# Repacing the load, norm and transposes of x, and moving small copies from VectorE to ScalarE, in a streaming-encoder layer

## The chip, the cores and the metric

The kernel runs on one core of one Trainium2 chip. The metric is the device time of one execution in microseconds. Before the change three runs gave 3767.56, 3769.85 and 3772.0 us, so the median is 3769.85 us.

## The reference, cut to what matters

One layer over 4096 tokens of width 1024, in float32. The input is normalised and projected once; half of the projected columns feed a differential softmax attention (group A), the other half an RWKV-7 recurrence (group B); both are gated, joined, projected and added to the input.

```python
xn = rms_norm(h, norm_g[l]); proj = xn @ w_in[l]
# group A: four heads, block-causal
p = softmax(q1 k1) - lam * softmax(q2 k2);  o_a = p @ v
# group B: eight heads; token shift of r, k, v, decay and a inputs
rwkv_in = z + (prev(z) - z) * shift_mu
# state S (64 x 64 per head), token by token
S_t = S_{t-1} diag(w_t) + (S_{t-1} (-kk_t)) (kk_t * a_t)^T + v_t k_t^T;  y_t = S_t r_t
h = h + concat([o_a, o_b]) @ w_out[l]
```

## The kernel before, in words

There are three phases. Phase 1 projects x and runs the recurrence, phase 2 is the attention, phase 3 the output projection. The change touches phase 1 alone.

Phase 1 walks over eight blocks of 512 tokens, in the order r0 a0 r1 a1 r2 a2 r3 r4 r5 r6 r7 a7 a6 a5 a4 a3, where r is the recurrence's share of the columns and a the attention's. A block's normalised, transposed input is held as a high part xh and a low part xl, so each product is three matmuls (mm3). Each letter is a row of jobs. A token-major job (VB and GB of r, V and GA of a) runs tm_part twice (L264), 16 steps each, a step being the three matmuls of one of eight weight tiles; its first part makes output rows of tokens 0 to 255 of the block, its second part those of 256 to 511. In each part two outputs s0 and s0+1 are interleaved, the second lagging by two steps. A feature-major job (fm_groups) takes 8 or 16 steps. Weight tiles come from a ring of eight; a tile's release, in part two of a token-major job, issues the load of the tile eight further on. After the first pass the weights come from a kept copy in DRAM (L233).

x for the next block is brought in beside the jobs: x_load (L148) loads two tiles into a ring of two buffers, x_norm (L157) squares them on ScalarE, takes the rsqrt on GpSimd and scales them on ScalarE, x_trans (L168) transposes them in four groups on TensorE (L176), and each group is evicted by ScalarE to xh (L179) and by VectorE to xl (L180). The first half of a block is normed and transposed in the last job before the block (x_norm0, x_half0), the second half in the block's first job (x_half1); `paced` (L317) runs each piece after given steps of the job.

Beside the projections run four streams, written as generators: p1_stream prepares units of 256 tokens (decay, keys, bonus; GpSimd makes rk at L506, TensorE the bonus sum from it at L524), p2_stream builds the chunk matrices and inverts them (the elimination on VectorE at L578 and L579, then the matmuls pz L594 and ptt L613 with copies Zs and TT), c_stream carries the state over chunks of 64 tokens (px L687, copy xs L690, pu L695, pst L716, state L725 and L728), o_stream finishes the output. The token shift of r, k and the LoRA columns is made in ev_shift (L285): ScalarE scales, VectorE adds the shifted rest, the first column from the carry and saves the last column as the new carry.

TensorE's instructions stand in the order in which the code issues them. After every step of the projections `tick` (L924) gives each stream a turn; a yield of n waits n beats, a negative yield also waits for a beat divisible by four (G). The other engines and SP's DMA queue are ordered by the framework's scheduler.

Of the kernel before, what the change touches and what calls it, by code (L numbers as in the profile page):

```python
# [12 lines left out]
AF = mybir.ActivationFunctionType  # L13
ALU = mybir.AluOpType
# [11 lines left out]
W = dict(  # L26
    G=4,    xn=2, xl=1024, sw=1024, np=2, le=3, l0=8, gb=5, pj=3, sb=4, wb=8, tb1=7, wm=0,
    xw=2048, cw=512, pl=1, pelat=330, tb=3, pb=3, lag2=2.0, ms=40, a0=2, a1=2, a2=2, a3=2,
    a4=2, a5=2, a6=2, a7=2, a8=2, a9=2, b0=2, b1=2, b2=2, b3=2, b4=2, b5=2,
    b6=2, b7=2, b8=1, b9=1, c0=10, c1=8, c2=2, c3=2, c4=1, c5=1, c6=2, c7=3,  # L30
    c8=2, o0=2, o1=4, o2=2, o3=4, o4=2, o5=2, o6=1, held=5, el=1, pz=18, ld=14,
    ba=2,  df=[2, 2, 2, 2],
# [76 lines left out]
def _phase1(ctx, tc, nc, e):  # L109
    x, w_in, norm_g, shift_mu = e["x"], e["w_in"], e["norm_g"], e["shift_mu"]  # L110
    S, D, KD, NB, NU = e["S"], e["D"], e["KD"], e["NB"], e["NU"]
# [34 lines left out]
    xraw = {}  # L146

    def x_load(b, t):  # L148
        xs = []
        for s in range(2):  # L150
            r0 = b * BT + t * 256 + s * 128
            xv = xp.tile([128, D], F32, tag="xv", name="xv", bufs=2)
            nc.sync.dma_start(xv, x[r0:r0 + 128, :])
            xs.append(xv)
        xraw[b, t] = xs
# [28 lines left out]
    jobs, tiles, first_tile = [], [], []  # L184
# [56 lines left out]
    def release(n):  # L241
        assert n == nuse[0], (n, nuse[0])
        nuse[0] += 1
        wt.pop(n)
        prep()

    def mm3(po, ah, al, bh, bl, k):
        nc.tensor.matmul(po, ah, bh, start=(k == 0), stop=False)  # L248
        nc.tensor.matmul(po, ah, bl, start=False, stop=False)  # L249
        nc.tensor.matmul(po, al, bh, start=False, stop=(k == KD - 1))  # L250
# [10 lines left out]
                yield  # L261
            evacs[p](po)

    def tm_part(n0, s0, evac, last, side_x):  # L264
        po = {}
        order = []
        for n in range(KD + 2):
            if n < KD:
                order.append((s0, n))
            if n >= 2:  # L270
                order.append((s0 + 1, n - 2))
        for s, k in order:
            if k == 0:
                po[s] = ps_j.tile([128, BT], F32, tag="pj", name="pjt")
            w = wt[n0 + k]
            sl = slice(128 * s, 128 * s + 128)
            mm3(po[s], xh[:, k, sl], xl[:, k, sl], w[:, 0].rearrange("p a c -> p (a c)"), w[:, 1].rearrange("p a c -> p (a c)"), k)
            if k == KD - 1:
                evac(s)(po[s])
            if last and s == s0 + 1:  # L280
                release(n0 + k)
            next(side_x, None)
            yield

    def ev_shift(gi, dst, t0):  # L285
        def f(po):
            o = stg.tile([128, 512], F32, tag="st", name="st")
            nc.scalar.activation(o, po, AF.Copy, scale=om_f[:, gi:gi + 1])
            mu = mu_f[:, gi:gi + 1]
            nc.vector.scalar_tensor_tensor(o[:, 1:512], in0=po[:, 0:511], scalar=mu, in1=o[:, 1:512], op0=ALU.mult, op1=ALU.add)  # L290
            nc.vector.scalar_tensor_tensor(o[:, 0:1], in0=carry[:, gi:gi + 1], scalar=mu, in1=o[:, 0:1], op0=ALU.mult, op1=ALU.add)
            nc.vector.tensor_copy(carry[:, gi:gi + 1], po[:, 511:512])
            nc.sync.dma_start(dst[:, t0:t0 + 512], o)
        return f

# [21 lines left out]
    def paced(g, steps):  # L317
        for n in range(64):
            if n in steps:
                next(g, None)  # L320
            yield

    def x_half1(b):
        x_norm(b, 1)
        yield
        yield from x_trans(b, 1)
        if b == 0:
            xfree[0] = True
            raw_next()

    def x_half0(b):
        yield from x_trans(b, 0)
        x_load(b, 1)
        yield

    def x_norm0(b):
        x_norm(b, 0)
        yield

    def tile_job(i, kind, parts, evs, nxt):  # L340
        n0 = first_tile[i]
        if kind == "f":
            assert not bg
            yield from fm_groups(n0, parts, [ev(0) for ev in evs])
            return
        half1 = bg.pop(1, None)
        assert half1 is None or nxt is None
        if nxt is not None:
            x_load(nxt, 0)
        if half1 is not None:  # L350
            side = paced(x_half1(half1), (4, 6, 8, 10, 12, 13))
        else:
            side = paced(x_norm0(nxt) if nxt is not None else iter(()), (10,))
        yield from tm_part(n0, 0, evs[0], False, side)
        for _ in side:
            pass
        side = paced(x_half0(nxt) if nxt is not None else iter(()), (1, 4, 7, 10, 11))
        yield from tm_part(n0, 2, evs[0], True, side)
        for _ in side:
            pass  # L360
        if nxt is not None:
            bg[1] = nxt
# [29 lines left out]
    order = []  # L392
# [4 lines left out]
    def main():  # L397
        x_norm(0, 0)
        yield from x_trans(0, 0)
        x_load(0, 1)  # L400
        bg[1] = 0
        for _ in range(RING):
            prep()
        for i, (k, parts, evs, nxt, rdone) in enumerate(jobs):
            yield from tile_job(i, k, parts, evs, nxt)
            if rdone:
                done_r[0] += 1
# [127 lines left out]
    def p2_unit(u):  # L535
# [39 lines left out]
        for j in range(31):  # L575
            n, w = 31 - j, j // 2 + 1
# [11 lines left out]
        TT = TTs[u % 2]  # L588
        pz = ps_g.tile([128, 16, 32], F32, tag="pg", name="pz")
        Drf = Dr.rearrange("p c r s -> p s c r")  # L590
        for pc in range(16):
            for h in range(2):
                b0 = 64 * h
# [3 lines left out]
            yield  # L597
        Zs = rq.tile([128, 16, 32], F32, tag="e2", name="Zs", bufs=3)
        nc.scalar.copy(Zs[32:64], pz[32:64])
        nc.vector.tensor_copy(Zs[96:128], pz[96:128])  # L600
        for q in range(4):
            sl = slice(32 * q, 32 * q + 32)
            nc.scalar.copy(TT[sl, :, 32 * (q % 2):32 * (q % 2) + 32], DT[sl])
# [5 lines left out]
        pt = ps_g.tile([128, 16, 32], F32, tag="pg", name="ptt")  # L609
        for pc in range(16):  # L610
            for h in range(2):
                b0 = 64 * h
                nc.tensor.matmul(pt[b0:b0 + 32, pc], Zs[b0 + 32:b0 + 64, pc], DT[b0 + 32:b0 + 64, pc], start=True, stop=True)  # L613
        yield W["b8"]
        nc.scalar.copy(TT[0:32, :, 32:64], pt[0:32])
        nc.vector.tensor_copy(TT[64:96, :, 32:64], pt[64:96])
        yield W["b9"]
        UN[u] = (ARF, WC, BON, RN, GS, bkt, TT)

# [30 lines left out]
    def c_stream():  # L650
# [5 lines left out]
        for ch in range(4 * NU):  # L656
# [3 lines left out]
            ARF, WC, BON, RN, GS, bkt, TT = UN[u]  # L660
# [22 lines left out]
            px, pu, pst = pc[:, 0], pc[:, 1], pc[:, 0]  # L683
# [3 lines left out]
                    nc.tensor.matmul(px[64 * h:64 * h + 64, j], GS[c][:, j, h, 0:64], svu[:, h, j], start=True, stop=True)  # L687
            yield W["c3"]
            xs = rp.tile([128, 4, 64], F32, tag="xs", name="xs", bufs=1)
            nc.vector.tensor_copy(xs, px)  # L690
            yield -W["c4"]
            for j in range(4):
                for h in range(2):
# [90 lines left out]
    def p1_stream():  # L784
        for u in range(NU):
            while done_r[0] * BT < 256 * (u + 1):
                yield 1
            p_load(u)
            yield W["ld"]
            yield from p1_unit(u)  # L790

    def p2_stream():
        for u in range(NU):
            yield from p2_unit(u)

    for n, (kind, b) in enumerate(order):
        ts = tiles_r(b) if kind == "r" else tiles_a(b)
        nb = order[n + 1][1] if n + 1 < len(order) else b
        for m, (cols, w, k, parts, evs) in enumerate(ts):
# [7 lines left out]
            nxt = nb if (m == len(ts) - 1 and nb != b) else None  # L807
# [18 lines left out]
    carry = c1.tile([128, 9], F32, name="carry")  # L826
# [88 lines left out]
    with tc.manual_schedule(engines={mybir.EngineType.PE}):  # L915
        side = [p1_stream(), p2_stream(), c_stream(), o_stream()]
# [535 lines left out]
```

## Time and profile before

| what | us |
|---|---|
| runs, median (of 3) | 3769.85 |
| profiled execution | 3761.58 |
| its span | 3759.9 |
| PE busy | 3609.4 (96%) |
| VectorE (DVE) busy | 2632.4 (70%) |
| ScalarE (ACT) busy | 1922.4 (51%) |
| GpSimd (POOL) busy | 761.2 (20%) |

PE is TensorE's matmuls, PEld its weight loads. An idle time is put down to what ended it: "PE pt L176 <- ACT xv L166" is time in which the transposes into pt waited for ScalarE's scaling of x. The granted clock is given as a share: 1.00 is 2.4 GHz, 0.50 is 1.2 GHz, and a mean in between says that a part of the stretch ran at 1.2 GHz. Phase 1 ends at about 2140 us, phase 2 at about 3600 us.

### The profile page before, as it was taken

What the parts mean: (1) busy time and instruction counts of PE and PEld (TensorE: products, weight loads), DVE (VectorE), ACT (ScalarE), POOL (GpSimd) and SP (SyncE); (2) the same over time, 40 slices, a digit from 0 to 9 for tenths busy, and PEclk for the clock granted to TensorE, in tenths of its full rate; (3) what the DMA queues carried; (4) which work ended last, traced back from release to release, by engine and by line L of the source; (5) the groups of instructions that cost most, each with busy time, mean ns of one, the idle gap of its engine ahead of it and who ended that gap; (6) DMA issues with size and microseconds to landing.
All of it is one profiled execution on the core that took longest, in us unless ns stands there. A gap on an engine that the chain in (4) does not pass through costs nothing.

```text
span 3759.9 us, 69957 instructions
## 1 busy us (share of the span) xinstructions
PE 3609.4 (96%) x26370; PEld 3050.9 (81%) x26370; DVE 2632.4 (70%) x5882; ACT 1922.4 (51%) x4042; POOL 761.2 (20%) x1156
## 2 busy tenths in 40 slices
PE   7999999999999999998999999999999999989999
PEld 5777777777777778777777789999999999978887
DVE  3566666667767787757777588898898898863333
ACT  4452352444445443444444377787787787761111
POOL 0112211211212222212221032222222222211000
PEclk9999999999999999999999999999999999999999
DMA  7976665666555565665675651141141131033332
GB/s 231 354 267 204 209 212 198 222 204 225 192 192 190 191 226 174 215 209 196 221 239 200 204 122 48 41 113 37 49 104 49 38 82 40 21 134 121 134 134 74
DMA packets 346092, 593.60 MB, mean 158 GB/s; under 512 B 55193, under 2 KB 210329, under 8 KB 345754
## 3 DMA queue, kind: packets, MB, share of 16 engines
q1 hardware_dynamic: 344602, 587.62, 48.4%
q8 instruction: 208, 3.41, 0.4%
q10 hardware_dynamic: 1152, 1.51, 0.1%
q14 instruction: 130, 1.06, 0.1%
HBM read 434.85 MB, written 154.14 MB: 157 GB/s over the span
## 4 chain that ended last, share of the span: by engine, by line
PE 75%; DVE 13%; DMA 4%; ACT 3%; issue 2%; SPq 2%; POOL 1%; DVEq 0%; POOLq 0%; ACTq 0%
PE po L1222 12%; PE ps L1127 6%; PE ps L1126 6%; PE tp L1197 6%; PE pjf L248 5%; PE pjf L250 4%; PE pjf L249 4%; PE pjt L248 4%; PE pjt L250 4%; PE pjt L249 4%; PE po L1372 3%; PE po L1371 3%; PE po L1370 3%; DVE DG L578 2%; DVE TL L579 2%
## 5 line engine op out<-in xcount | busy, mean ns | idle before, releaser
L1159 ACT ACTIVATE ring<-ring,nm 128x2048 f32<-128x2048 f32 (+14 forms) x472 | 589.0, 1253 | 31.3 <-DVE nm L1151 30.2
L1141 DVE CUSTOM_DVE_ANT_0 ring<-ps,zcol 128x1024 f32<-128x1024 f32 (+6 forms) x464 | 485.2, 1058 | 109.2 <-PE ps L1127 103.1
L1222 PE MATMUL po<-v,pt 128*128 128x128 f32 x4224 | 539.5, 276 | 10.0 <-ACT pt L1210 5.4
L1222 PEld LDWEIGHTS po<-v,pt 128*128 128x128 f32 x4224 | 517.9, 192 | 28.5 <-ACT pt L1210 7.3
L1126 PE MATMUL ps<-k,ta 128*128 128x512 f32 (+3 forms) x1152 | 483.1, 420 | 7.3 <-DMA ta<-q_d 4.9
L248 PE MATMUL pjt<-w,xh 128*128 128x512 f32 x1024 | 436.2, 426 | 29.1 <-DMA w<-ws_d 13.4
L248 PE MATMUL pjf<-xh,w 128*128 128x512 f32 x1088 | 451.1, 415 | 6.0 <-ACT w L236 4.5
L1127 PE MATMUL ps<-k,tb 128*128 128x512 f32 (+3 forms) x1152 | 432.0, 379 | 0.0
L250 PE MATMUL pjf<-xh,w 128*128 128x512 f32 x1088 | 431.0, 396 | 0.5 <-DVE w L237 0.5
L249 PE MATMUL pjf<-xl,w 128*128 128x512 f32 x1088 | 429.9, 395 | 0.0
L249 PE MATMUL pjt<-w,xh 128*128 128x512 f32 x1024 | 410.5, 401 | 0.9 <-DVE w L237 0.9
L250 PE MATMUL pjt<-w,xl 128*128 128x512 f32 x1024 | 410.0, 401 | 0.1
L1182 DVE SCALAR_TENSOR_TENSOR ring<-ring,rho 128x512 f32<-128x512 f32 (+3 forms) x600 | 407.1, 702 | 1.6
L1210 ACT COPY pt<-tp 128x512 f32<-128x512 f32 (+3 forms) x576 | 303.1, 550 | 194.0 <-PE tp L1197 188.7
L1197 PE MATMUL tp<-ident,ring 128*128 128x128 f32 x2112 | 313.6, 274 | 3.7 <-DVE ring L1182 3.7
L1197 PEld LDWEIGHTS tp<-ident,ring 128*128 128x128 f32 x2112 | 254.6, 142 | 40.6 <-issue 3.7
L248 PEld LDWEIGHTS pjt<-w,xh 128*128 128x128 f32 x1024 | 199.0, 194 | 80.9 <-DMA w<-ws_d 20.3
L248 PEld LDWEIGHTS pjf<-xh,w 128*128 128x128 f32 x1088 | 207.3, 191 | 57.4 <-ACT w L236 6.5
L250 PEld LDWEIGHTS pjf<-xh,w 128*128 128x128 f32 x1088 | 207.0, 190 | 49.2 <-DVE w L237 2.7
L1126 PEld LDWEIGHTS ps<-k,ta 128*128 128x128 f32 x1152 | 219.2, 190 | 32.8 <-issue 5.0
L1127 PEld LDWEIGHTS ps<-k,tb 128*128 128x128 f32 x1152 | 220.1, 191 | 23.4
L249 PEld LDWEIGHTS pjf<-xl,w 128*128 128x128 f32 x1088 | 208.0, 191 | 38.1
(205 smaller groups left out, 6421.4 us busy)
## 6 DMA issues: line engine op xcount, KB each, us to landing
w<-ws_d SPq DMA_DIRECT2D x448, 512.0 KB, 5.3
ws_d<-w SPq DMA_DIRECT2D x64, 512.0 KB, 5.3
xv<-in_x_dram SPq DMA_DIRECT2D x48, 512.0 KB, 5.4
ta<-q_d SPq DMA_DIRECT2D x128, 128.0 KB, 2.9
tb<-q_d SPq DMA_DIRECT2D x128, 128.0 KB, 3.0
k<-k_d SPq DMA_DIRECT2D x32, 512.0 KB, 7.1
mi<-mix_d SPq DMA_DIRECT2D x32, 512.0 KB, 3.3
xi<-in_x_dram SPq DMA_DIRECT2D x32, 512.0 KB, 4.2
```

Of the source, the lines that this page charges most:

```text
L248: nc.tensor.matmul(po, ah, bh, start=(k == 0), stop=False)
L249: nc.tensor.matmul(po, ah, bl, start=False, stop=False)
L250: nc.tensor.matmul(po, al, bh, start=False, stop=(k == KD - 1))
L1126: nc.tensor.matmul(ps[:, c:c + w], rr(ta[:, m, qs]), rr(k[:, m, c:c + w]), start=True, stop=False)
L1127: nc.tensor.matmul(ps[:, c:c + w], rr(tb[:, m, qs]), rr(k[:, m, c:c + w]), start=False, stop=True)
L1141: nc.vector.tensor_tensor_reduce(rg(m, ro, x), st["ps", b, m][:, c - 1024 * b:c - 1024 * b + x], msk, 0.125, -3.0e38, ALU.add, ALU.max, ac ...
L1159: nc.scalar.activation(rg(m, ro, x), rg(m, ro, x), AF.Exp, bias=st["nm"][:, m:m + 1], accum_out=st["lp"][:, m, j:j + 1])
L1182: nc.vector.scalar_tensor_tensor(rg(0, ro, x), in0=rg(1, ro, x), scalar=st["rho"], in1=rg(0, ro, x), op0=ALU.mult, op1=ALU.add)
L1197: nc.tensor.transpose(tp[:, j], rg(0, c, 128), ident)
L1210: nc.scalar.copy(pt[:, :n], st.pop(("tp", g))[:, :n])
L1222: nc.tensor.matmul(st["po"], pt[:, j], vt[h, kb // 8][:, kb % 8], start=(kb == 0), stop=(kb == i))
L1370: nc.tensor.matmul(po, mh[:, k], wh[k][:, fs], start=(k == 0), stop=False)
```

## The change

- The load of the next block's first half is issued one job earlier where the weights of that job come from the kept copy, and its norm then runs after step 3 of the job instead of step 10. Its transposes run after steps 0, 3, 5 and 8 of part two instead of 1, 4, 7 and 10, and the second half's load after 9 instead of 11.
- The second half's norm runs after step 5 instead of 4 and its transposes after steps 12, 14, 17 and 20 of the job instead of 6, 8, 10 and 12 (for the first block as before).
- Part two of a token-major job lags its second output by four steps instead of two.
- The yield before the bonus matmul (a8) is 5 instead of 2.
- Four kinds of small operations go from VectorE to ScalarE: the copy xs, the first column and the carry in ev_shift, and the second halves of the copies Zs and TT.

```diff
-    a4=2, a5=2, a6=2, a7=2, a8=2, a9=2, b0=2, b1=2, b2=2, b3=2, b4=2, b5=2,
+    a4=2, a5=2, a6=2, a7=2, a8=5, a9=2, b0=2, b1=2, b2=2, b3=2, b4=2, b5=2,
...
-    def tm_part(n0, s0, evac, last, side_x):
+    def tm_part(n0, s0, evac, last, side_x, lag):
...
-        for n in range(KD + 2):
+        for n in range(KD + lag):
             if n < KD:
                 order.append((s0, n))
-            if n >= 2:
-                order.append((s0 + 1, n - 2))
+            if n >= lag:
+                order.append((s0 + 1, n - lag))
...
-            nc.vector.scalar_tensor_tensor(o[:, 0:1], in0=carry[:, gi:gi + 1], scalar=mu, in1=o[:, 0:1], op0=ALU.mult, op1=ALU.add)
-            nc.vector.tensor_copy(carry[:, gi:gi + 1], po[:, 511:512])
+            nc.scalar.activation(o[:, 0:1], carry[:, gi:gi + 1], AF.Identity, scale=mu, bias=o[:, 0:1])
+            nc.scalar.copy(carry[:, gi:gi + 1], po[:, 511:512])
...
+        if half1 is not None:
+            side = paced(x_half1(half1), (5, 12, 14, 17, 20, 21) if half1 else (4, 6, 8, 10, 12, 13))
+        elif nxt is not None:
+            if (nxt, 0) not in xraw:
+                x_load(nxt, 0)
+                side = paced(x_norm0(nxt), (10,))
+            else:
+                side = paced(x_norm0(nxt), (3,))
+        else:
+            side = iter(())
+        yield from tm_part(n0, 0, evs[0], False, side, 2)
         if nxt is not None:
-            x_load(nxt, 0)
-        if half1 is not None:
-            side = paced(x_half1(half1), (4, 6, 8, 10, 12, 13))
-        else:
-            side = paced(x_norm0(nxt) if nxt is not None else iter(()), (10,))
-        yield from tm_part(n0, 0, evs[0], False, side)
-        for _ in side:
-            pass
-        side = paced(x_half0(nxt) if nxt is not None else iter(()), (1, 4, 7, 10, 11))
-        yield from tm_part(n0, 2, evs[0], True, side)
+            for _ in side:
+                pass
+            side = paced(x_half0(nxt), (0, 3, 5, 8, 9))
+        yield from tm_part(n0, 2, evs[0], True, side, 4)
...
         for i, (k, parts, evs, nxt, rdone) in enumerate(jobs):
+            if i + 1 < len(jobs) and jobs[i + 1][3] is not None and not tiles[min(first_tile[i + 1], len(tiles) - 1)][3]:
+                x_load(jobs[i + 1][3], 0)
...
-        nc.vector.tensor_copy(Zs[96:128], pz[96:128])
+        nc.scalar.copy(Zs[96:128], pz[96:128])
...
-        nc.vector.tensor_copy(TT[64:96, :, 32:64], pt[64:96])
+        nc.scalar.copy(TT[64:96, :, 32:64], pt[64:96])
...
-            nc.vector.tensor_copy(xs, px)
+            nc.scalar.copy(xs, px)
```

## Rows read from the trace of the kernel before

**Rows 1.** Table by windows, phase 1: stretch, length, busy us of each engine, clock, DMA.
```profile
220.00:2140.00 1920.00, 1827.27 (x15083) 1476.65 (x15081) 1322.98 (x2967) 802.83 (x1806) 412.56 (x410) 0.98 0.63 207
```

**Rows 2.** PE's waits, 220 to 2140: who waited for whom, us, times, longest.
```profile
PE pt L176 <- ACT xv L166: 19.8, 15, 4.1
PE pjt L248 <- DMA w<-ws_d: 13.4, 12, 2.9
PE pbn L524 <- POOL rr L506: 13.3, 3, 5.2
PE pt L176 <- DVE xl L180: 11.9, 5, 4.5
PE pjt L248 <- DVE st L311: 11.7, 7, 4.0
```

**Rows 3.** Table by windows, slices of 20 us around waits for x and rk.
```profile
500.00:520.00 20.00, 17.32 (x87) 14.41 (x85) 18.47 (x50) 14.60 (x34) 3.14 (x6) 0.89 0.75 278
...
1400.00:1420.00 20.00, 16.15 (x185) 13.13 (x186) 10.03 (x19) 10.10 (x25) 4.13 (x4) 0.83 0.37 122
1620.00:1640.00 20.00, 19.70 (x142) 16.16 (x143) 8.87 (x15) 11.24 (x29) 1.41 (x3) 0.87 0.52 152
1960.00:1980.00 20.00, 16.64 (x126) 13.54 (x125) 17.97 (x41) 7.56 (x18) 3.30 (x2) 0.91 0.70 239
```

**Rows 4.** Timeline, PE and ACT, 502 to 517: start, us, engine, line, operation.
```profile
502.88 0.60 PE L176 MATMUL pt<-ident,xv 128*128 128x128 f32 x4
...
514.00 0.33 PE L176 MATMUL pt<-ident,xv 128*128 128x128 f32 x1 [0.37 <-ACT xv L166]
515.41 1.17 ACT L166 ACTIVATE xv<-xv,rs 128x1024 f32<-128x1024 f32 x1
516.63 0.90 PE L176 MATMUL pt<-ident,xv 128*128 128x128 f32 x3 [2.30 <-ACT xv L166]
```

**Rows 5.** Groups by line and shape, DVE and ACT, 0 to 2140: busy, mean ns, idle before.
```profile
L690 DVE COPY xs<-pc 128x256 f32<-128x256 f32 x64 | 26.8, 418 | 31.3 <-PE pc L687 31.0
L291 DVE SCALAR_TENSOR_TENSOR st<-carry,mu_f,st 128x1 f32<-128x1 f32 x72 | 18.1, 252 | 0.0
L600 DVE COPY Zs<-pz 32x512 f32<-32x512 f32 x16 | 11.2, 697 | 84.9 <-ACT Zs L599 84.7
L179 ACT ACTIVATE xh<-pt,g_t 128x256 fp32r<-128x256 f32 x192 | 87.9, 472 | 91.6 <-DVE xl L180 50.6 <-PE pt L176 39.7
L489 ACT ACTIVATE f<-tha,kac,kah 128x256 f32<-128x256 f32 x64 | 35.5, 604 | 0.2
```

**Rows 6.** Timeline, PE, bonus matmuls and pz, 1284 to 1404.
```profile
1284.58 1.87 PE L524 MATMUL pbn<-rks,rr 128*128 128x2 f32 x8 [4.75 <-POOL rr L506]
1291.65 1.98 PE L594 MATMUL pz<-Dr,GS 32*32 32x32 f32 x64 [0.40 <-DVE Dr L586]
1403.85 1.87 PE L524 MATMUL pbn<-rks,rr 128*128 128x2 f32 x8 [5.19 <-POOL rr L506]
```

**Rows 7.** Timeline, ACT and DVE, the two half copies of pz, 542 to 544.
```profile
542.63 0.58 ACT L599 COPY Zs<-pz 32x512 f32<-32x512 f32 x1
543.24 0.70 DVE L600 COPY Zs<-pz 32x512 f32<-32x512 f32 x1 [11.45 <-ACT Zs L599]
```

**Rows 8.** Timeline, ACT and DVE, one eviction of the token shift, 1269 to 1279.
```profile
1269.31 0.67 ACT L288 ACTIVATE st<-pjf,om_f 128x512 f32<-128x512 f32 x1
1278.55 0.75 DVE L290 SCALAR_TENSOR_TENSOR st<-pjf,mu_f,st 128x511 f32<-128x511 f32 x1
```

**Rows 9.** The last chunk, timeline of PE and DVE; then SP's waits: us, times, longest.
```profile
2123.59 0.69 PE L687 MATMUL pc<-svu,GS 128*64 128x64 f32 x16
2132.66 0.87 DVE L728 TENSOR_TENSOR svu<-svu,WC 64x256 f32<-64x256 f32 x2
SPq L1025 <- DVE svu L728: 11.8, 1, 11.8
```

## The prediction

> **What bounds the kernel now.** I read the page's slices first, then the table by windows, then PE's waits, then short timelines around the longest of them. The change touches phase 1 alone (0 to about 2140 us); the stretch after it is written by its own planner and stays as it is. From 220 to 2140 us PE is busy 1827 of 1920 us, with DVE at 1323 and ACT at 803 [rows 1]: PE is the bound, and what can be won is its 93 us of idle time and what it loses at the lower clock. So the question is which waits end last on PE. They are few and named [rows 2]: the transposes of x wait for the normalised x (19.8 us, 15 times) and for a buffer that VectorE's xl frees (11.9), the projections wait for weights (13.4) and for a PSUM buffer that the gate's eviction frees (11.7), and the bonus matmul waits for GpSimd's rk (13.3, three times). A long wait costs twice: in 500 to 520 us the granted clock has a mean of 0.89, and so on in six such 20 us slices around waits for x, of which [rows 3] has the first and the last; 20 us x (1 - clock) over the six (0.89, 0.85, 0.88, 0.95, 0.91, 0.87) is 13.0 us of PE's work lost at 1.2 GHz.
>
> **The order of the work.** PE runs in written order, in beats of three matmuls: a 32-step job of the token-major kind is 32 beats. From the last transposes of one half of x to the first of the next half are 12 beats, and they took 514.00 - 502.88 = 11.1 us [rows 4], so a beat with its share of the side streams is 0.93 us. I use that price for a beat throughout.
>
> **The change, part by part.**
>
> *x repaced.* The second half of x is loaded when the first half's last transposes free its buffers. From those transposes (502.88) to the second scaled tile (515.41 + 1.17 = 516.58) are 13.7 us [rows 4]; the order gives 12 beats = 11.1 us, so PE waits 2.3 us more and loses its clock. Now the first half's last transposes stand at step 8 of part two instead of 10, and the second half's first at step 12 of the next job instead of 6: 20 beats = 18.6 us against 13.7. The wait is covered with 4.9 us to spare, in all ten transitions with this distance. It removes 19.8 + 13.0 = 32.8 us. What is late next: the second half is used from step 16 on, so its transposes at 12, 14, 17, 20 have only 3 to 4 beats (2.8 to 3.7 us) to be evicted, where before they had 10 or more. An eviction is ScalarE 0.472 us [rows 5] and then VectorE, two of each in turn, so about 2 us when nothing stands before them. With VectorE behind, the matmuls wait instead. From below this costs nothing, from above all of the 32.8 comes back; nearest is the case where queues are short, with some 0.8 us lost in each of ten transitions: 8. Net **25**. The earlier load of the first half and its earlier norm I cost at nothing: its transposes are not the ones that wait in [rows 4], and the early DMA stands on SP ahead of stores that it doesn't hold up, since its buffers are free by then. If it did hold SP, later weights would be late (below). The first half's own transposes come in 0, 3, 5, 8, a little denser than before; where they wait for VectorE (11.9 us in [rows 2]) nothing is relieved, **-1**, with -5 and +3 as ends.
>
> *Lag 4 in part two.* The first output of part two ends at step 11 instead of 13 and the second starts two steps later, so an eviction has two beats (1.9 us) more before its buffer is wanted. Of the seven waits for the gate's eviction (11.7 us, the longest 4.0) this can take at most 1.9 each; the longest stand where VectorE is behind and come back at the next wait. Take **+5** of 0 to 11.7. Against it: the weights of the job are released later, the first after step 6 instead of 4, the next job of the same kind uses them from 16 on, so the load has 8 beats (7.4 us) at the tightest place instead of 10. Fifteen such boundaries x 1.9 = 28 us is the upper end, 0 the lower; most of the twelve waits for weights come from SP standing behind stores, not from a late release: **-4**.
>
> *The bonus matmul four beats later (a8).* Slots come at every fourth beat, so the distance from rk to the matmul grows from 6 beats to 10, and for the second pair of heads all stands 8 beats (7.4 us) later. The three waits are 4.75, 5.19 and 3.36 us, so all end. But at 1284.58 the next matmul that needs VectorE's inverse waited 0.40 us right after [rows 6]: there VectorE is the bound, and the 4.75 would be waited out at 1291.65. The other two count: 5.19 + 3.36 = 8.6, and the clock around them (0.83 and 0.91 [rows 3]: 3.4 + 1.8 = 5.2) makes 13.8; **+12** of 0 to 18. The price: all of the inverse and the recurrence moves 8 beats later against the projections. At the end of phase 1 this isn't hidden. Now the last chunk's first matmul is at 2123.59 and its state is done at 2132.66 + 0.87, 1.5 us before the projections end at about 2135 [rows 9]. Shifted by 8 beats, the last two steps of the chain have no projections beside them, and SP's first loads of phase 2 wait for that state (11.8 us at one load, [rows 9]). Ends 0 and 7.4; the chain without its filler matmuls is shorter by some 2, so **-5**. Elsewhere the shift makes new meetings of busy VectorE with x, with either sign; take **-5** of -20 to +10.
>
> *Copies to ScalarE.* VectorE loses 64 copies of xs (26.8 us), 72 first columns (18.1), 16 halves of Zs (11.2), and the like halves of TT and the carries: the three rows alone are 56 us of 1323 [rows 5]. ScalarE gains 64 x 0.472, 32 x 0.58, and 72 x two tiny ones. For the first column with two pointer operands no row exists; it lies between 0 and the 0.604 us of a 256-column activation with two such operands [rows 5], I take 0.4, by that row and its smaller size. All in all under 126 us on an engine that is 42% busy: no bound there. What VectorE wins off PE's path is worth little: **+2**, ends 0 and 8. The half copies stood one after the other already: VectorE's half began at 543.24, when ScalarE's 0.58 us from 542.63 were over [rows 7]. So nothing parallel is given up, and ScalarE's second half is 0.1 us shorter.
>
> The Trainium skill, "PSUM — Partial Sum Buffer", in "PSUM bank collisions raise a hardware error", lets two engines read one bank at once if they are in different quadrants of partitions; by that the halves could have run side by side and the move would cost 16 x 2 x about 0.5 us of the chain. The trace doesn't agree: the halves are strictly one behind the other.
>
> *The wait that is added.* The carry's copy reads the same PSUM tile as VectorE's shift. If ScalarE has to wait for that, its queue stands still, and behind it stand xs, the tanh and exp of the next unit, and the copies for the inverse. One shift began at 1278.55 for a ScalarE eviction that ended at 1269.98: 9.3 us to its end [rows 8]. That is the worst; after most evictions ScalarE is idle for some us anyway. Take **-4**; the ends are 0 and the rival below.
>
> The same section of the Trainium skill keeps any two engines apart on one bank and quadrant, reads against reads too. By that rule this wait exists; [rows 5] has ScalarE's xh waiting 50.6 us for VectorE's xl of the same tile, which agrees.
>
> **Sum.** 25 - 1 + 5 - 4 + 12 - 5 - 5 + 2 - 4 = 25 us. The profiled execution took 3761.58 (span 3759.9), so 3736.6 by it; it lay 8.3 under the median of the runs shown (3769.85), and against that median the forecast is **3745**.
>
> **The rivals.**
>
> *Forecast, 0.55*: 3745, own range 3730 to 3757.
>
> *The wait moves from x to its eviction, 0.18.* The transposes are in time, but the projections wait for xl with the same clock loss. For it: 3 to 4 beats, and VectorE at 18.47 of 20 us in the slice of [rows 3]. Against it: shorter waits. The 25 shrink to 5: 3765.
>
> *ScalarE's queue, slower, 0.13.* The carry's copy holds ScalarE until VectorE's shift, p1's tanh and exp start late, rk is late again and PE waits at the bonus matmul as now at 1403.85. Each such wait costs 5.2 and 3.4 of clock = 8.6 us. Units 7 to 9 have their elimination beside r jobs, six halves: 6 x 8.6 = 52, so 3745 + 52 = 3797. It decides from the third half on (3 x 8.6 = 26 eats the gain). Against it: the matmul stands 4 to 8 beats later. The rule of the Trainium skill above is what makes this rival, and its chance is the 0.13.
>
> *Weights, 0.04.* Lag 4 makes most of the fifteen boundaries wait: 20 of the 28 us are paid, 3761 to 3765.
>
> *All of it comes, 0.10.* No eviction is late and the counter-costs stay near 0: 50 us, 3720.
>
> **How the numbers follow.** A measurement tells 0.2%, 7.5 us, from no change. Faster (under 3762): nearly all of the forecast (0.53), all of the last rival, 0.07 of the second: 0.70. Same: 0.02 of the forecast, 0.09 of the second, the weights, a little of ScalarE's queue: 0.16. Slower: 0.14, from ScalarE's queue and the worst of the second. The range goes from the good case to just beyond no change: 3718 to 3777.
>
> **What would show it.** Right: the waits of PE for the scaled x fall to under 3 us after 220, those for rk to under 3, the mean clock of 220 to 2140 rises, PE's new waits for xl at the projections stay under 10 us in total, and phase 2's first scores start some 5 us later after the projections' end than now. Wrong: waits for xl at the projections of 15 us or more, PE waiting for ScalarE's xs or Zs, ScalarE idle before the carry's copy for long and rk late again, or weights late at the boundaries of token-major jobs.

## The result, and the profile after

The change made the kernel slower: 3789.5 us median (3788.6 to 3790.3) against 3768.7 for the kernel before, ratio 1.0054 [1.0036, 1.0071]. The forecast was 3745 with a range to 3777, so both the sign and the range were missed. The profiled execution has a span of 3786.8 us. Kernels are compared by their ratios below: executions of one kernel lie up to 22 us apart, and the profiled one of before (3761.58) was 8 us under the median of its own, so two traces alone would say +27.

Lines beyond 410 are 7 further down than before (pz is L601, px L694, xs L697); kernels with x's old places keep the old numbers. The table by windows, phase 1 (columns as in [rows 1]):

```profile
220.00:2160.00 1940.00, 1829.55 (x15090) 1473.46 (x15086) 1259.39 (x2739) 869.58 (x2027) 411.76 (x408) 0.97 0.61 204
```

PE does the same work in 20 us more. VectorE lost 64 us of busy time and ScalarE gained 67, as the copies should make it; the mean clock did not rise but fell a little. PE's idle time is 1940 - 1829.6 = 110 us, where [rows 1] has 93. The waits of PE in that stretch tell where it sits (waited for: us, times, longest us):

```profile
PE pjt L248 <- DMA w<-ws_d: 29.5, 26, 3.8
PE pjt L248 <- DVE st L311: 12.5, 5, 4.1
PE pa L465 <- DVE xl L180: 8.4, 4, 2.7
PE pjt L250 <- DVE xl L180: 8.3, 8, 2.0
PE ptt L620 <- ACT Zs L606: 7.4, 3, 4.6
...
PE pt L176 <- DVE xl L180: 5.7, 3, 2.6
PE pjt L248 <- DVE sl L301: 5.2, 1, 5.2
...
PE pjt L248 <- ACT carry L292: 3.7, 1, 3.7
PE pc L702 <- ACT xs L697: 2.8, 1, 2.8
PE pjt L248 <- ACT xh L179: 2.5, 2, 1.6
PE pt L176 <- ACT xv L166: 2.5, 1, 2.5
```

Against [rows 2]: what the change aimed at is gone (x's norm 19.8 to 2.5, rk 13.3 to nothing). In its place stand weights (13.4 to 29.5), x's evictions at the projections and at pa, which is the next unit's inner products (16.7 together, neither of them among the long waits before), the inverse's copies on ScalarE (7.4), and two evictions of projections (sl and carry, 8.9). With the transposes' waits for xl (11.9 to 5.7) these three are 37 us that went. Over all of PE's waits in the two windows 46 us went and 67 came.

The end of phase 1, timeline of PE and DVE (start us, us, engine, line, operation, idle before):

```profile
2154.66 0.39 PE L250 MATMUL pjt<-w,xl 128*128 128x512 f32 x1
...
2157.31 0.69 PE L723 MATMUL pc<-svu,bkt 128*64 128x64 f32 x16 [1.35 <-DVE svu L719]
...
2158.95 0.87 DVE L735 TENSOR_TENSOR svu<-svu,WC 64x256 f32<-64x256 f32 x2
...
2166.34 0.76 PE L1133 MATMUL ps<-k,ta 128*128 128x512 f32 x1 [6.58 <-DMA ta<-q_d]
```

The projections end at 2155.1, 20.0 us later than before (2135.1). The last chunk's state is done at 2158.95 + 0.87 = 2159.8, now behind them, and the first full score matmul of phase 2 starts 11.2 us after the projections' end where it was 5.3. These 6 us are the price that the forecast had put at 5. So the handover came as predicted, and in these two executions the projections were 20 us late instead of early. By the ratio, which has 20 us in all, it is some 14.

The moved copies, groups by line and shape (busy, mean ns, idle before):

```profile
L291 ACT ACTIVATE st<-carry,st,mu_f 128x1 f32<-128x1 f32 x72 | 27.9, 388 | 1.4
...
L697 ACT COPY xs<-pc 128x256 f32<-128x256 f32 x64 | 23.7, 371 | 10.3 <-PE pc L694 9.3
...
L292 ACT COPY carry<-pjf 128x1 f32<-128x1 f32 x72 | 11.3, 157 | 62.5 <-DVE st L290 60.8 <-DVE DG L585 0.3
...
L607 ACT COPY Zs<-pz 32x512 f32<-32x512 f32 x16 | 9.2, 578 | 0.4
```

Beside [rows 5]: xs costs 371 ns for 418, the half of Zs 578 for 697, the first column 388 for 252 (the forecast took 400). The wait that was added is there: ScalarE stood 60.8 us before the carry's copy for VectorE's shift. The Trainium skill, "PSUM — Partial Sum Buffer", in "PSUM bank collisions raise a hardware error", keeps two engines from reading one bank and quadrant together; the trace agrees that the copy waits, and the next section shows that this wait is not what made the kernel slower.

### The profile page after: what moved, and what is told of

The parts are those of the page before. It is cut to its first block, busy times and chain, and to the rows that moved or that the text cites. A ratio compares the mean times of both kernels' runs of the same rounds, so it can differ in the third digit from the quotient of the medians.

```text
span 3786.8 us, 70039 instructions
## 1 busy us (share of the span) xinstructions
PE 3613.9 (95%) x26370; PEld 3048.8 (81%) x26370; DVE 2566.6 (68%) x5642; ACT 1993.0 (53%) x4282; POOL 763.4 (20%) x1156
## 4 chain that ended last, share of the span: by engine, by line
PE 69%; DVE 13%; DMA 5%; ACT 3%; issue 2%; POOL 1%; SPq 0%; DVEq 0%; POOLq 0%; ACTq 0%
PE po L1229 12%; PE ps L1134 6%; PE ps L1133 6%; PE tp L1204 6%; PE pjt L248 4%; PE pjf L248 4%; PE pjt L250 3%; PE pjt L249 3%; PE pjf L250 3%; PE pjf L249 3%; PE po L1379 3%; PE po L1378 3%; PE po L1377 3%; DVE TL L586 2%; DVE DG L585 2%
## 5 line engine op out<-in xcount | busy, mean ns | idle before, releaser
L248 PE MATMUL pjt<-w,xh 128*128 128x512 f32 x1024 | 439.5, 430 | 60.6 <-DMA w<-ws_d 29.5
L250 PEld LDWEIGHTS pjt<-w,xl 128*128 128x128 f32 x1024 | 199.3, 195 | 60.9 <-DVE xl L180 16.4
```

## The experiments

The change has four parts: the copies, x's places, lag 4 and the shift (a8=5, by which the bonus matmul stands 4 beats later and the inverse and the recurrence 8). Eighteen kernels were run. The table gives each one's parts, its ratio to the kernel before, the end of the last projection, and the time from there to the first full score matmul, both in its profiled execution. That one lies up to 7 us from its kernel's median, and 8 under it for the kernel before, so a few us in the column of the last projection tell nothing.

| kernel | copies | x | lag 4 | shift | ratio [95%] | last projection us | to phase 2 us |
|---|---|---|---|---|---|---|---|
| before | | | | | 1 | 2135.1 | 5.3 |
| p_act | yes | | | | 0.9973 [0.9962, 0.9983] | 2131.8 | 5.1 |
| f_x | yes | yes | | | 0.9962 [0.9949, 0.9976] | 2132.5 | 5.2 |
| f_lag | yes | | yes | | 0.9978 [0.9966, 0.9990] | 2131.0 | 4.9 |
| f_a8 | yes | | | yes | 0.9990 [0.9981, 0.9999] | 2133.7 | 12.0 |
| m_a8 | yes | yes | yes | | 0.9968 [0.9957, 0.9979] | 2130.6 | 4.3 |
| m_x | yes | | yes | yes | 0.9979 [0.9970, 0.9988] | 2129.6 | 11.1 |
| m_lag | yes | yes | | yes | 1.0018 [1.0009, 1.0027] | 2148.8 | 11.5 |
| after | yes | yes | yes | yes | 1.0054 [1.0036, 1.0071] | 2155.1 | 11.2 |
| m_act | | yes | yes | yes | 1.0074 [1.0061, 1.0087] | 2164.0 | 11.7 |
| p_x | | yes | | | 1.0007 [0.9995, 1.0020] | 2142.3 | 5.0 |
| p_lag | | | yes | | 1.0004 [0.9992, 1.0016] | 2138.3 | 4.5 |
| p_a8 | | | | yes | 1.0024 [1.0013, 1.0034] | 2145.8 | 11.4 |

**Each part taken out of the full change.** The theory on record was that one part carries the loss. The edits on the changed kernel:

```diff
 m_lag: -    yield from tm_part(n0, 2, evs[0], True, side, 4)
        +    yield from tm_part(n0, 2, evs[0], True, side, 2)
 m_a8:  -a8=5,
        +a8=2,
 m_x:   -(5, 12, 14, 17, 20, 21) if half1 else (4, 6, 8, 10, 12, 13)
        +(4, 6, 8, 10, 12, 13)
        -side = paced(x_half0(nxt), (0, 3, 5, 8, 9))
        +side = paced(x_half0(nxt), (1, 4, 7, 10, 11))
        -                x_load(jobs[i + 1][3], 0)      # the early load
 m_act: -nc.scalar.copy(xs, px)
        +nc.vector.tensor_copy(xs, px)                  # and the other copies likewise
```

> The changed kernel (3789.5 us) with part two's lag at two steps again, all else as changed. Theory W (late weights): lag 4 releases the weights later, and PE's waits for weights grew by 16 us with their clock; then this run is 12 to 20 us faster than the changed kernel, about 3772, and PE's waits for weights after 220 us fall from 30.6 us to under 18. Theory A (ScalarE's queue) and theory S (the eight-beat shift of a8): within 6 us of the changed kernel.

> The changed kernel with a8 back at 2, so that the inverse and the recurrence stand eight beats earlier again. Theory S: the shift costs the 6 us at the end of phase 1 and bad meetings before; this run is 10 to 20 us faster than the changed kernel, and the waits for rk come back only in part. Theory W: it is 0 to 8 us faster, the end of phase 1 alone, less the waits for rk (13 us) that return; so about the same, 3785 to 3792.

> The changed kernel with the old places of load, norm and transposes of x (lag 4, a8 and the ScalarE copies stay). Theory X (the repace itself is the loss, by xl late at the projections and by x's load standing ahead of weights on SP): 8 to 20 us faster than the changed kernel, with the waits for weights in the first jobs of a block gone. Theories W, A, S: 10 to 30 us slower than the changed kernel, since the waits for the scaled x (19.8 us and their clock) come back.

> The changed kernel with the five copies back on VectorE. Theory A: ScalarE's queue makes Zs (7.4 us), xs (2.8) and the carry (3.7 + 1.8) late and with the clock some 15 us; this run is 10 to 20 us faster than the changed kernel. Theories W, S, X: within 6 us of it.

Out of 1.0054, taking out the shift gives 32 us back, x's places 28, lag 4 14, and the copies cost 8 more when they are undone: the first two are each worth more than the whole loss of 20, and the first three together 74. So no part carries it alone. What lag 4 does in the full change is seen in PE's waits of the kernel without it:

```profile
PE pjt L248 <- DVE st L311: 34.9, 12, 6.1
PE pjt L248 <- DMA w<-ws_d: 12.5, 15, 2.8
```

With lag 4 these were 12.5 and 29.5: it takes 22 us from the waits for the eviction and puts 17 on the weights, whose buffers come free later. The forecast had +5 and -4, so the direction was right and both sizes were several times too small.

**Each part alone on the kernel before.**

```diff
 p_a8:  -a8=2,
        +a8=5,
 p_x:   x's steps, early load and early norm as in the change, lag 2, a8=2, copies on VectorE
 p_lag: -def tm_part(n0, s0, evac, last, side_x):
        +def tm_part(n0, s0, evac, last, side_x, lag):   # 2 in part one, 4 in part two
 p_act: -nc.vector.tensor_copy(xs, px)
        +nc.scalar.copy(xs, px)                          # and the other copies likewise
```

> The kernel before with a8 = 5 alone. Taken out of the changed kernel it gave back 33 us. If the eight-beat shift costs by itself (phase 1's end and p1's later matmuls against the other streams), this run is 5 to 25 us slower than before although the waits for rk (13.3 us) go. If it costs only together with the new places of x (p1's matmuls then wait for a buffer that x holds), this run is within 6 us of before or faster.

> The kernel before with the new places of x alone (lag 2, a8 = 2, copies on VectorE). My prediction gave it 25 us of gain. If it is good by itself and bad only beside a8: 3740 to 3760. If its own new waits (xl at the projections, x's load ahead of weights) eat it: 3763 to 3785.

> The kernel before with lag 4 in part two alone. Taken out of the changed kernel it gave back 14 us. If weights are late by themselves: 5 to 15 us slower than before, with PE's waits for weights up from 15 to 25 us or more and the waits for the gate's eviction down from 11.7. If they are late only beside x's new load: within 5 us of before.

> The kernel before with the five copies on ScalarE alone. Taken out of the changed kernel they made it 7 us slower, so they help there. If that holds alone: 3755 to 3767. If ScalarE's queue costs by itself (the rival of the prediction): 3775 or more, with waits of PE for Zs, xs and the carry of over 10 us.

The copies gain 10 us, x's places and lag 4 nothing that can be measured, the shift loses 9. Added up the four alone would make +3, and the kernel has +20. That x's places alone bring nothing is read from PE's waits in p_x:

```profile
PE pjt L248 <- DMA w<-ws_d: 16.6, 16, 3.0
PE pt L176 <- DVE xl L180: 13.0, 5, 5.9
...
PE pjt L248 <- ACT xh L179: 8.5, 4, 2.6
PE pjt L250 <- DVE xl L180: 8.0, 5, 2.8
...
PE pc L702 <- DVE xs L697: 4.1, 2, 2.4
PE ptt L620 <- DVE Zs L607: 2.9, 3, 1.9
```

The wait for x's norm is down from 19.8 to 1.5, as the forecast had it, but the projections now wait for the two evictions of the same transposes (16.5 us, not among the waits before) and smaller ones fill the rest. The reason is in the records of L176 and L180. Each of the four groups of transposes makes a pair of tiles, and from its last transpose to the end of its second xl the second half of x took 3.6 us in the mean of 44 pairs, in before (up to 7.7) and in p_x (up to 8.1) alike. The new places give the four pairs 3, 3, 4 and 5 whole beats in PE's order at lag 2; three are 2.8 us. The first two pairs of p_x took 4.6 and 4.7 us in the mean, and nearly all of the 16.5 us stand at steps 16 and 17, where the first pair is used. One of these waits, timeline of ACT, DVE and PE in p_x:

```profile
531.73 0.48 DVE L180 SCALAR_TENSOR_TENSOR xl<-pt,g_t,xh 128x256 fp32r<-128x256 f32 x1
531.74 2.50 ACT L610 COPY TT<-DT 32x512 f32<-32x512 f32 x4 [2.86 <-DVE DT L591]
...
532.27 0.51 PE L250 MATMUL pjt<-w,xl 128*128 128x512 f32 x1 [2.75 <-DVE xl L180]
...
535.39 0.79 PE L248 MATMUL pjt<-w,xh 128*128 128x512 f32 x1 [2.62 <-ACT xh L179]
```

The first xl comes late on VectorE, and before the pair's second xh four copies of the inverse hold ScalarE for 2.50 us.

In p_a8 PE waits longer for x's norm (19.8 before) and for the gate's eviction (11.7 before), and the handover shows by itself (PE's waits; 4.9 before):

```profile
PE pt L176 <- ACT xv L166: 26.5, 19, 4.9
PE pjt L248 <- DVE st L311: 21.0, 9, 5.6
...
PE ps L1126 <- DMA ta<-q_d: 6.8, 1, 6.8
```

**VectorE relieved.** If VectorE's being busy makes the new waits, the change should pay once VectorE has less to do. Both kernels lose every second step of the elimination, at unchanged beats.

```diff
         for j in range(31):
+            if j % 2:
+                yield W["el"]
+                continue
             n, w = 31 - j, j // 2 + 1
```

> The kernel before without VectorE's work in every second step of the elimination (its yields stay; 15 of 31 steps are left out of the inverse). Theory D (VectorE's lateness is what PE's waits are made of, wherever PE's order puts them): PE's waits for VectorE and GpSimd after 220 us (xl, the gate's eviction, svu, rk: 46.7 us) fall below 20, those for the scaled x by half, and the run takes 3715 to 3735. Theory O (the places in PE's order, the PSUM ring and the weights make them): 3750 or more.

> The changed kernel with the same 15 steps left out of the elimination. Theory D: with VectorE in time the change gives what I forecast, less phase 1's end, so this run is equal to or faster than the kernel before with the same steps left out (3700 to 3735), the waits for weights staying at 20 us or more. Theory O: it stays 12 to 25 us slower than that one.

0.9900 [0.9885, 0.9915] and 0.9977 [0.9968, 0.9987]: both are faster, and the gap between them is 29 us, not smaller than the 20 of the full kernels. VectorE is busy 107 us less in each, of 1323 and 1247 (220 to 2140). The theory fell: the loss does not shrink with VectorE's load. In the relieved kernel with the change PE still waits 24.8 us for weights and 13.3 us for xl at the projections.

**Two that missed their aim.**

```diff
 h_end: -            yield -W["a8"]
        +            yield -(W["a8"] if u < 15 else 2)
 w_x12: -side = paced(x_half0(nxt), (0, 3, 5, 8, 9))
        +side = paced(x_half0(nxt), (0, 3, 5, 8, 12))
```

> The changed kernel with a8 = 2 in the last unit alone, so that the recurrence ends eight beats earlier and nothing before the last unit moves. If the end of phase 1 costs what the trace shows (first full scores 5.3 us after the last projection in the kernel before, 11.3 in the changed one): 5 to 8 us faster than the changed kernel. If something else sets phase 2's start, such as the stores ahead of its loads on SP: within 3 us.

> The changed kernel with the load of x's second half after step 12 of part two instead of 9. In the changed kernel its 1 MB goes ahead of the third weight tile of the next job on SP's queue, and that tile comes late five times (1.7 to 3.0 us). If this order is what makes the weights late: those five waits go, the scaled x waits a little (2 to 3 us a transition, at most), and the run is 5 to 12 us faster than the changed kernel. If lag 4's later release alone does it: the third tile stays late and the run is within 4 us of it or slower.

h_end was to bring the end of phase 1 forward, but by the count of beats the last chunk stays where it was, since steps are rounded up to every fourth beat. What moved is the last unit's bonus matmul, which then waited 3.3 us for rk. At 1.0074 [1.0059, 1.0089] it says nothing on the handover.

w_x12 was to set x's load behind the weights on SP, and did not. The issues of SP's queue, from the change and then from w_x12, at one such place:

```profile
511.60 2.14 SPq L233 DMA_DIRECT2D w<-ws_d  x2
515.38 0.81 SPq L153 DMA_DIRECT2D xv<-in_x_dram  x2
516.28 4.00 SPq L233 DMA_DIRECT2D w<-ws_d  x4
```

```profile
517.93 2.53 SPq L233 DMA_DIRECT2D w<-ws_d  x2
522.08 0.81 SPq L153 DMA_DIRECT2D xv<-in_x_dram  x2
522.98 2.94 SPq L233 DMA_DIRECT2D w<-ws_d  x4
```

All issues on SP and all work on VectorE, ScalarE and GpSimd stand in the same order in the two profiles, so whether x's load ahead of the weights makes them late is not tested by it. x's new places are not needed for it: m_x, with the old ones, waited 29.8 us for weights. As a second run of the same order, w_x12 shows how far one order varies: the ratio came again (1.0055 [1.0040, 1.0070]), but its last projection ends at 2163.7 us for 2155.1, and pa's waits are 11.0 us for 8.4.

**The remaining corners, and two more beats for x.** With these the copies are on ScalarE in all eight combinations of the other three.

```diff
 f_x:   change with lag 2 and a8=2
 f_lag: change with x's old steps and loads, a8=2
 f_a8:  change with x's old steps and loads, lag 2
 h1_early: -(5, 12, 14, 17, 20, 21) if half1
           +(5, 10, 12, 15, 18, 19) if half1
```

> Before with the copies on ScalarE and x's new places, without lag 4 and without the eight-beat shift. With the copies alone the ratio was 0.997, with copies, x's places and lag 4 it was 0.997. If the loss belongs to the meeting of x's places with the shift, x's places do no harm here: 0.996 to 0.998. If x's places lose wherever lag 4 doesn't help them, 1.000 or more.

> Before with the copies on ScalarE and lag 4, x's old places, no shift. Without interaction 0.997 like the copies alone. If lag 4's late weights are what loses (waits for weights went from 14.9 to 24.9 us with lag 4 alone), 0.999 or more, and weights over 22 us; if its later eviction is worth something beside the copies, 0.995.

> Before with the copies on ScalarE and the eight-beat shift, x's old places, lag 2. The sum of the two alone (-12 and +9) is 0.9995. If the shift only costs what it delays at the end of the projections (5 to 10 us), 0.998 to 1.000 and the last projection within 5 us of that of the copies alone. If the shift loses beside the projections too, even without x's new places: 1.002 or more.

> The full change with the transposes of x's second half two beats earlier (steps 10, 12, 15 and 18 for 12, 14, 17 and 20; the load has 18 beats or 16.7 us for the 13.7 it needs). If the new waits are those of an eviction that gets 3 or 4 beats and takes 3.8 us in the mean, the eight waits of the projections for xl (8.3 us) fall under 3 and the clock loss with them: 1.0015 to 1.003. If it is the shift that puts the next unit's inner products between x's transposes, the four waits of these for xl (8.4 us) stay over 5 and the ratio stays at 1.004 to 1.006. If x's load is late again, waits for xv over 8 us.

In us of 3770 against the kernel before: nothing else -10, x -14, lag -8, shift -4, x and lag -12, lag and shift -8, x and shift +7, all +20. Without the shift x's places gain 4 at either lag, within the uncertainty. With it they lose 11 at lag 2 and 28 at lag 4. Of the eight only the two in which x's places and the shift stand together are slower than before. Why lag 4 adds to their loss is in part in PE's order: it also brings the use of x's second half forward, so that the four pairs have 3, 3, 2 and 3 whole beats instead of 3, 3, 4 and 5. Of the projections' waits for xl 5.9 us are for the last two pairs in the change, and 2.1 in m_lag.

h1_early, 1.0035 [1.0023, 1.0048], lies between the two theories. Its waits:

```profile
PE pa L465 <- DVE xl L180: 10.7, 4, 4.0
...
PE pjt L250 <- DVE xl L180: 3.7, 2, 2.0
```

Two beats more halve the waits of the projections for xl (8.3 to 3.7), which is the short eviction, but pa's stay (8.4 to 10.7). By the ratios the kernel is 7 us faster than the change, with intervals that overlap; its profiled execution, in which the projections end at 2155.8, lies 7 us above its median and can't be set beside that of the change. The short eviction is a part at most, not the whole.

**Where the shift puts things.** One of pa's waits, timeline of ACT, DVE and PE in the changed kernel:

```profile
535.83 2.49 ACT L610 COPY TT<-DT 32x512 f32<-32x512 f32 x4
...
538.34 0.84 ACT L179 ACTIVATE xh<-pt,g_t 128x256 fp32r<-128x256 f32 x2
538.85 0.88 DVE L180 SCALAR_TENSOR_TENSOR xl<-pt,g_t,xh 128x256 fp32r<-128x256 f32 x2 [1.79 <-ACT xh L179]
...
539.48 0.36 PE L465 MATMUL pa<-wah,lrh 128*128 128x256 f32 x1 [1.34 <-DVE xl L180]
```

The inverse's four copies hold ScalarE for 2.49 us; x's xh stands behind them, VectorE's xl is idle 1.79 us for xh, and pa waits for the PSUM buffer that these free (pa and x's transposes draw on the same three, L128). The same four copies held x's second xh in p_x, without the shift; what the shift adds here is pa behind them. By the count of beats the shift moves the inner products in blocks 1 to 3 from step 4 of the job that carries x's second half to step 16, between the new transposes at 14 and 17. Three of pa's four waits are there (265.00, 539.48 and 803.16 us), each behind these four copies. If it is the place and not the lateness, a further shift of eight beats should repair it (by PE's order it brings these products to step 28, behind the last of the transposes; the step -4 of the expectation is the place of the products before them):

```diff
 a9:     -a8=5,
         +a8=9,
 a8_h1e: -a8=5,
         +a8=2,
         -(5, 12, 14, 17, 20, 21) if half1
         +(5, 10, 12, 15, 18, 19) if half1
```

> The full change with the bonus matmul's distance set to 9 instead of 5: by the order of beats the inverse and the recurrence stand 8 beats later again, and the next unit's inner products in blocks 1 to 3 go from step 16 to step -4 of the job that carries x's second half. If it is that meeting, the waits of these products for xl (8.4 us) fall under 3, the last projection ends at 2135 to 2145 instead of 2155, and the end of the program, which gets another 7 us at the handover, comes at 1.002 to 1.005. If later is simply worse, the last projection ends after 2160 and the ratio is 1.007 to 1.012.

> The full change without the shift (0.9968 before) and with the transposes of x's second half two beats earlier (10, 12, 15, 18). There the projections waited 11.7 us for xl; with two beats more for each eviction under 4 us of that stay, and with the clock 8 to 12 us come off: 0.994 to 0.995. If the eviction's lateness comes back at the next wait, as waits have done in this kernel, 0.996 to 0.9975.

a9 came at 0.9983 [0.9972, 0.9994], 27 us faster than the change, with the inverse and the recurrence later than there. The last projection ends at 2122.3, earlier than in any kernel of the table (the profiled execution is 5 us under its median), and phase 2 starts 17.4 us behind it. "Later is worse" fell, and the expectation was still too cautious (2135 to 2145, and a ratio of 1.002 to 1.005). PE's waits in a9, 220 to 2160:

```profile
PE pjt L248 <- DMA w<-ws_d: 21.5, 29, 2.4
PE ptt L620 <- ACT Zs L606: 14.3, 4, 6.2
PE pjt L250 <- DVE xl L180: 8.5, 6, 3.6
...
PE ps L1133 <- DMA ta<-q_d: 6.7, 1, 6.7
PE pt L176 <- DVE xl L180: 6.6, 4, 2.9
...
PE pjt L248 <- DVE st L311: 6.1, 2, 3.4
...
PE pa L465 <- DVE xl L180: 2.6, 2, 1.4
```

pa's waits fell under 3 us as expected, and with them the waits for weights (29.5 to 21.5) and for the gate's eviction (12.5 to 6.1). The inverse's wait for ScalarE doubled, which shows that this order has meetings of its own. In one stretch of block 2, 495 to 660 us, first the changed kernel and then a9 (columns as in [rows 1]):

```profile
495.00:660.00 165.00, 151.00 (x1111) 120.13 (x1110) 106.61 (x252) 68.24 (x159) 28.29 (x28) 0.99 0.57 193
```

```profile
495.00:660.00 165.00, 157.14 (x1248) 125.40 (x1247) 99.82 (x241) 72.39 (x168) 25.40 (x25) 0.99 0.60 203
```

At the same clock PE does 6.1 us more work in the same 165 us. Over all of phase 1 after 220, PE's idle time is 87 us in a9 and 108 in the change, and the trace's clock records have 75 us at the lower level of 1.2 GHz for 106. That is 21 us of waits and at most 15 of clock, for 33 that the projections end earlier.

a8_h1e at 0.9965 [0.9948, 0.9981] is not told apart from m_a8 (0.9968) or f_x (0.9962): the projections' waits for xl fell from 11.7 to 5.2, and the transposes' rose from 16.9 to 20.0, in a profiled execution 7 us above its median. The expected 0.994 to 0.995 did not come. These three are the fastest versions, some 13 us under before and 33 under the change; p_act (0.9973) lies within their intervals.

## Why the prediction was wrong

Parts put in one after the other, in us against the kernel before, beside the terms of the forecast (minus is faster; each measured step has an uncertainty of some 5 us):

| step | forecast | measured | from |
|---|---|---|---|
| copies to ScalarE, carry's wait | +2 | -10 | 1 to 0.9973 |
| x repaced, both halves | -24 | -4 | 0.9973 to 0.9962 |
| lag 4 | -1 | +2 | 0.9962 to 0.9968 |
| shift | -2 | +32 | 0.9968 to 1.0054 |
| sum | -25 | +20 | |

The split depends on the order. Beside the copies and lag 4 alone the shift costs nothing (0.9978 to 0.9979), and x's places put in last cost 28 (0.9979 to 1.0054): the loss belongs to the two together.

- **The step that failed most**: "Elsewhere the shift makes new meetings of busy VectorE with x, with either sign; take -5 of -20 to +10". The shift costs 32 us in this kernel, with x's new places in it. Six are the handover, as predicted (5.3 to 11.2 us, by a term of -5). It does end the waits for rk, which stood at 10.0 us in m_a8. The new meetings beside the projections therefore cost 32 - 6 + 10 = 36, far outside the ends. They were priced as noise because one shift was thought like another. They are particular places: eight beats more (a9) give 27 us back. And with 107 us less work on VectorE the loss stayed (el_after); in the meeting shown it was ScalarE's queue.
- **x repaced, net 25**: the removal of the 19.8 us was right, the price of what is late next was not. "About 2 us when nothing stands before them" was the price of the instructions; the records of before had 3.6 us in the mean for the same step. The cover was counted too long as well: the transposes stand behind the matmuls of their step, so PE's order leaves 2 to 3 whole beats with lag 4, where the forecast had 3 to 4 (and the transitions are eleven, not ten). Both were there to be counted before. So the forecast's second rival, the wait that moves from x to its eviction, is what happened to x's places.
- **The 13.0 us of clock** counted on top of x's waits didn't come: the time at 1.2 GHz from 220 us to the last projection was 92 us before, 89 in p_x, where these waits are gone, and 106 in the change.
- **Lag 4**: the net near nothing was right at this place in the order (in the full change it costs 14), by luck, since two terms were each too small; that lag 4 also shortens the cover of x's second half was left out.
- **The bonus matmul, +12**: the waits for rk are gone, as forecast, but the same shift pays more elsewhere.
- **Copies**: the gain of 10 (8 in the full change) was put at 2. The rival that ScalarE's queue makes the kernel slower, 3797, came close in time and was wrong in cause: rk is never late again, and undoing the copies makes the kernel slower still.
- **Weights**: forecast as a rival of 0.04 and only by lag 4's late release; they took 16 us more, and p_lag's 21.9 us (before 13.4) shows that lag 4 alone does half of it.

Of the forecast's own signs, x's norm, rk, the projections' waits for xl (8.3 us) and the handover came as it had them for being right; only the clock did not. The waits that came instead were ones that it had listed for being wrong (weights, Zs and xs, ScalarE's stand before the carry) or had not listed (pa and sl).

What stays open: which of the meetings carries how much of the 27 us between the change and a9 (pa's own waits are 6 of them), and where in the trace the copies' 10 us come from. VectorE no longer stands 84.7 us before its half of Zs [rows 5], but in p_act it stands at the next instruction that needs PE:

```profile
DVE GS L556 <- PE pgg L551: 119.9, 25, 16.3
```

That wait was 44.3 us before. PE's idle time up to the last projection is 87 us there and 88 before, but the two profiled executions took the same time (3761.2 and 3761.6 us), so these traces can't show the 10.

## What to carry to other kernels

In a program whose engines run in a written order, a shift of one stream against another is no small correction: price it by laying both orders side by side and listing what falls on the same buffers and queues, and try two or three shifts, since the next one may be 27 us better. Take the time that a buffer is held from the records of its whole life (last write to last read), not from the duration of the instructions that read it. Before a run is read as a test, see in its trace that the edit moved the order which it was to move: that of w_x12 moved nothing. Test parts of a change in pairs before they are put together: here three that cost nothing or little alone lose together, and leaving the shift out of the four makes the kernel 0.3% faster than before.

## What the runs showed that was not expected

- PE's idle time in phase 1 after 220 stays at 87 to 111 us in all thirteen kernels of the table, whichever wait is removed. Only in the kernel before with half of the elimination left out does it fall to 74.
- The interval from the last projection to the first full score is set by the shift alone: 4.3 to 5.7 us at a8=2, 10.9 to 12.0 at a8=5, 17.4 at a8=9, in every kernel, some 6 us for each eight beats of 0.93 us.
- On ScalarE the moved copies from PSUM were shorter than on VectorE (371 ns for 418, 578 for 697), the carry's copy took the same (157 for 152), and only the one-column update with two pointer operands was longer (388 for 252).
